# A hybrid decoder step: the first MLP product by seven block products in place of eight

## The chip, the core and the metric

The kernel runs on one core of one Trainium2 chip. TensorE (PE in the profile) multiplies, VectorE (DVE) and ScalarE (ACT) do the element-wise work, GpSimd (POOL) a little, and SyncE (SP) issues nearly all transfers. The metric is the time of one execution on the device in microseconds (us), the median of several runs.

## The reference

One layer of a decoder for 512 prompt tokens and 8 sample tokens that share the weights. What matters here, with all in fp32:

```python
u = rmsnorm(x, norm1_g) * (1 + sc1) + sh1
proj = u @ w_in                       # 1024 x 10272, split into nine sections
...
dt = softplus(dt_raw + dt_bias)       # dt_raw: 32 columns of proj
...
x = x + g1 * (merged @ w_o)
u2 = rmsnorm(x, norm2_g) * (1 + sc2) + sh2
hmid = square(relu(u2 @ w_mlp1))      # 1024 x 4096
x = x + g2 * (hmid @ w_mlp2)          # 4096 x 1024
y = rmsnorm(x, norm_f_g)
```

## The kernel before

**Layout.** Activations lie transposed: 128 features on the partitions, T = 520 tokens (512 prompt, 8 sample) along the row, so that a 1024-wide activation is eight tiles. A product goes by *windows*: one window computes one block of 128 output features for all 520 tokens, over eight blocks of 128 input features.

**Precision.** Each fp32 operand is split into a high part (fp32r, written by an ACT copy) and a low part (what is left, by a DVE subtraction): `wh`, `wl` for weights, `hi`, `lo` for activations. A product of two blocks is three matmuls: high by high, high by low, low by high. As 520 tokens are two halves of 260 columns (two PSUM banks), a window has 8 x 3 x 2 = 48 matmuls.

**Order.** Every engine works through its instructions in the order in which the program writes them; there is no scheduler. The main loop takes window `n` in four quarters `q` of 12 matmuls each. Around them it places the evacuation of window `n - 1` out of PSUM, the weight split of window `n + 2` (ACT copy, then DVE subtraction), and *hooks*: functions that `at(q, w, fn)` has put at a quarter of a window, and that `run` calls, sorted within one quarter by `PLAN["order"]`. Two two-bank accumulators (`mmtile`) are in rotation and four single banks (`aux`). Weights arrive in tiles of 1 MB for two windows (`load_w`, three buffers), issued on SP six windows ahead. Split weights have three buffers.

**The start.** Windows 0 to 3 compute sections B and C of the scan branch. An evacuation (`xbc_evac`) reads the accumulator twice on ACT (`raw`, `cv`) and runs a short convolution on DVE; a `finish` some windows later adds the sample columns (DVE) and applies SiLU (ACT). The softplus of `dt` is a chain of some fourteen small DVE instructions, `dt_b2`, hooked at the last quarter of window 3; `dt_b` comes before it, and `dt_c` (PE, ACT, DVE) in window 5 needs its result. `dt_b2` and the finish of window 2 stand in the same quarter, `dt_b2` first.

**The MLP** is in two halves of 2048 hidden features: sixteen windows `m1` (first product, then relu, square and split of the hidden tile), then sixteen windows `m2` (second product, two windows for each of eight output blocks, one accumulator; then `m2_evac` adds to the residual). The first nine `m1` windows use an input that isn't normalized yet, with nine more columns (270 in the second half of a row) that carry the shift; the others use `u3`, the normalized input that hooks prepare meanwhile (`make_u2`, `make_u2_lo`).

**The end.** The last output block is computed in two parts of the tokens, so that its residual, transposes (`finish_tile`), row sums (`last_rstd`) and stores overlap.

Of the kernel before, what the change touches and what calls it, by code (L numbers as in the profile page):

```python
# [8 lines left out]
F32 = mybir.dt.float32  # L9
# [8 lines left out]
P = 128  # L18
# [40 lines left out]
 'rstd': 11,  # L59
 'rstd_s': 17,  # L60
 'dt': [1, 3, 10],
 'u3': 9,
 'make_u2': 6,
 'lo_u2': 4,
 'hm': [1, 3],
 'last': [0, 2]}

# [5 lines left out]
def tile_hybrid_step(  # L73
# [32 lines left out]
    def act(name, dtype=F32):  # L106
        return ap.tile([P, SLOT], dtype, name=nm(name), tag="act", bufs=NSLOT)
# [4 lines left out]
    def small(shape, name):  # L112
        return sp.tile(shape, F32, name=nm(name), tag="small", bufs=4)
# [7 lines left out]
    def halves(ap_):  # L121
        return ap_.rearrange("p (h c) -> p h c", h=2)
# [16 lines left out]
    def a_copy(out, in_, func=AF.Copy, **kw):  # L139
        S.activation(out=out, in_=in_, func=func, **kw)  # L140

    def mm(out, lhsT, rhs, start=True, stop=True):
        PE.matmul(out, lhsT=lhsT, rhs=rhs, start=start, stop=stop)  # L143


    xa = {}
# [105 lines left out]
    def win(mat, r0, c0, i, xs, evac=None, first=True, last=True, n1=TH):  # L252
        wins.append(((mat, r0, c0), i, xs, evac, first, last, n1))
# [24 lines left out]
    def split_w(n):  # L278
# [8 lines left out]
            tt(lo, src, hi.bitcast(F32), ALU.subtract)  # L287
        rests.append(rest)

    def half(ps, h):  # L290
        return ps[h] if isinstance(ps, list) else ps[:, h, :]

    def product_part(ps, n, ks, h):
        hi, lo = splits[n]
        xs, first, last = wins[n][2](), *wins[n][4:6]
        c0, c1 = PART[h]
        for k in ks:
            xh, xl = xs[k]
            for i, (w_, x_) in enumerate(((hi, xh), (hi, xl), (lo, xh))):
                mm(ps[:, 0, 0:c1 - c0], w_[:, k, :], x_[:, c0:c1], first and k == 0 and i == 0,  # L300
                   last and k == KT - 1 and i == 2)

    def product(ps, n, ks):
# [17 lines left out]
    def at(q, w, fn, *args):  # L321
        hooks.setdefault(4 * w + q, []).append((fn, args))
# [242 lines left out]
    def rstd_small(v, n, r, rows=P):  # L565
        q = small([P, n], "q")[0:rows]
        a_copy(r, v, AF.Sqrt)
        V.reciprocal(out=r, in_=r)
        stt(q, r, -0.5, r, ALU.mult, ALU.mult)
        tt(q, q, v, ALU.mult)  # L570
        stt(r, q, 1.5, r, ALU.add, ALU.mult)
# [95 lines left out]
        mg.append(split(s))  # L667


    x2, u2, u3 = [], [], []  # L670
    sq2 = {}

    def residual(x_, xo, ps, prm, o):
# [33 lines left out]
        spread(rx, 1, 0, sq2[1])  # L707


    hm = []  # L710

    def make_u2(k):
        us, v, hi = small([P, NS], "us"), act("v2"), act("hi", F32R)
# [6 lines left out]
        a_copy(hi[:, 0:NP], v[:, 0:NP], AF.Identity, bias=mp(3, k))  # L720
        a_copy(hi[:, NP:T], v[:, NP:T])
        u3.append((v, hi))

    def make_u2_lo(k):
        v, hi = u3[k]
        lo = act("lo", F32R)
        stt(lo[:, 0:NP], v[:, 0:NP], mp(3, k), hi.bitcast(F32)[:, 0:NP], ALU.add, ALU.subtract)
        G.tensor_tensor(out=lo[:, NP:T], in0=v[:, NP:T], in1=hi.bitcast(F32)[:, NP:T], op=ALU.subtract)
        u3[k] = hi, lo

    def m1_evac(ps, w):
        if w >= W_U3:
            r = act("relu")
            a_copy(halves(r[:, 0:T]), ps[:, :, 0:TH], AF.Relu)
            at(PLAN["hm"][0], cur[0], m1_square, r)
            return
# [27 lines left out]
    def m2_evac(ps, w, o, half):  # L764
        residual(x2[o], x2[o], ps, 5, o)
        if half:
            if o == 0:
                sqf.insert(0, act("sqf"))
            add_square(sqf[0], x2[o], o == 0)
            if o == KT - 2:  # L770
                V.memset(vf, 1.0)
                at(end, w + 1, row_means, sqf, 1.0 / D, vf)
            at(mid, w + 1, finish_tile, o)

    sqf = []
    vf = const([P, 5], "vf")
    rf = const([P, 5], "rf")


    def last_evac(ps, h):  # L780
        o, (c0, c1) = KT - 1, PART[h]
        x_ = x2[o]
        stt(x_[:, c0:min(c1, NP)], ps[:, 0, 0:min(c1, NP) - c0], mp(5, o), x_[:, c0:min(c1, NP)])
        if not h:
            t = small([P, NS], "rs")
            tt(t, ps[:, 0, NP - c0:T - c0], msm(5, o), ALU.mult)
            tt(x_[:, NP:T], t, x_[:, NP:T], ALU.add)
            sqf.insert(0, act("sqf"))
        a_copy(sqf[0][:, c0:c1], x_[:, c0:c1], AF.Square)

    def last_rstd(h):
        cs = PART_C[h]
        row_means(sqf[0:1], 1.0 / D, vf, vf, cs)
        a, b = cs[0], cs[-1] + 1
        rstd_small(vf[:, a:b], b - a, rf[:, a:b])

    def last_out(h):
# [70 lines left out]
    W_U3 = W_M + PLAN["u3"]  # L868
# [75 lines left out]
    at(2, W_M, norm2_r)  # L944
    at(0, W_M + 1, norm2_b)
    for k in range(KT):
        at(PLAN["make_u2"] + 4 * k, W_M, make_u2, k)
        at(PLAN["make_u2"] + 4 * k + PLAN["lo_u2"], W_M, make_u2_lo, k)
    at(end, W_M + 4, load_g)

    cur = [0]
# [2 lines left out]
        firsts.setdefault(wn[0], n)  # L954
    load_order = sorted(firsts, key=lambda k: firsts[k])
    state = {"load": 2, "split": 3}

    def loads_to(n):
        while state["load"] < len(load_order) and firsts[load_order[state["load"]]] <= n:
# [1 line left out]
            state["load"] += 1  # L961

    def splits_to(n, whole=True):
        while state["split"] < NW and state["split"] <= n:
            split_w(state["split"])
            state["split"] += 1
        while whole and rests:
            rests.pop(0)()
# [270 lines left out]
        wins[n][3](ps_of.pop(n), n)  # L1239
        splits_to(3 + n)  # L1240
    dt_a()
    for n in range(3, NW - 2):
        cur[0] = n
        loads_to(n + 6)
        early = n < 40
        for q in range(4):
            if q == (1 if n == W_M + 1 else PLAN["evac" if early else "evac2"]) and wins[n - 1][3]:
                wins[n - 1][3](ps_of.pop(n - 1), n - 1)
            if q in PLAN["split" if early else "split2"]:
                splits_to(n + 2, q == PLAN["split" if early else "split2"][1])  # L1250
            if q == 0:
                ps_of[n] = mmtile("ps") if wins[n][4] else ps_of.pop(n - 1)
            product(ps_of[n], n, (2 * q, 2 * q + 1))
            for w in ([2, 3] if n == 3 and q == mid else [1, 2, 3] if n == 3 and q == end else [n]):
                run(w, q)


    cur[0] = NW - 2
    splits_to(NW - 1)
    wins[NW - 3][3](ps_of.pop(NW - 3), NW - 3)  # L1260
    for h in range(2):
        ps = mmtile("ps")
        for q in range(4):
            n = NW - 2 + q // 2
            product_part(ps, n, range(4 * (q % 2), 4 * (q % 2) + 4), h)
            run(NW - 2 + h, q)
            if h and q == PLAN["last"][0]:
                finish_tile(KT - 1, PART_C[0])
                last_rstd(0)
            if h and q == PLAN["last"][1]:  # L1270
                last_out(0)
        last_evac(ps, h)
    finish_tile(KT - 1, PART_C[1])
    last_rstd(1)
    last_out(1)

# [30 lines left out]
```

## Time and profile before

| | |
|---|---|
| three runs | 1166.93, 1167.24 (median), 1168.3 us |
| the profiled execution | 1167.75 us, of which 1165.9 us lie between the first and the last instruction (the span) |
| PE busy | 98% of the span, 9688 matmuls |
| DVE busy | 724.2 us, 62% |
| ACT busy | 448.2 us, 38% |
| DMA | 164.95 MB, mean 141 GB/s |
| granted clock of PE | 0.996 in the mean |

All rows come from that one execution. A row of the timeline gives the start, the time from the first start to the last end of so many like instructions, and in brackets how long the engine had been idle and what ended it. Like instructions overlap, so that the time of two is less than twice the time of one.

### The profile page before, as it was taken

Reading aid. Unit: us, or ns where it says so; the run is one execution under the profiler, and the core shown is the slowest. Engines: PE = TensorE matmul, PEld = TensorE weight load, DVE = VectorE, ACT = ScalarE, POOL = GpSimd, SP = SyncE. Lnnn points to the kernel's source line nnn. Section 1 sums busy time; section 2 is a strip of 40 time slices with the busy share of each in tenths; the row PEclk is TensorE's granted clock in tenths of the full one; section 3 lists DMA queues with packets and bytes.
Section 4 is the critical chain, followed back from the end, with each engine's and each line's share of the span. In section 5 each row is a group of like instructions: output and inputs, shape, how many; then the busy total and the mean of one; then the engine's idle time right before and its main releaser. Section 6 shows DMA issues by size and latency. Waiting matters only on the chain.

```text
span 1165.9 us, 22851 instructions
## 1 busy us (share of the span) xinstructions
PE 1142.0 (98%) x9688; PEld 1111.9 (95%) x9688; DVE 724.2 (62%) x1340; ACT 448.2 (38%) x666; POOL 42.4 (4%) x93
## 2 busy tenths in 40 slices
PE   7989999999999999999999999999999999999997
PEld 5789999999999888999999999999999999999997
DVE  5767888778888587888566333677743233444443
ACT  4446555455552222234443222345532113333222
POOL 3001111011110000000000000001000000000000
PEclk9989999999999999999999999999999999999999
DMA  9924333333348996566563243333322323232211
GB/s 284 321 73 132 114 114 96 93 112 114 114 141 283 333 324 201 181 187 198 183 229 100 97 163 122 115 123 101 100 73 90 117 85 108 74 109 73 73 37 74
DMA packets 137745, 164.95 MB, mean 141 GB/s; under 512 B 7144, under 2 KB 107961, under 8 KB 137636
## 3 DMA queue, kind: packets, MB, share of 16 engines
q1 hardware_dynamic: 137116, 162.85, 43.1%
q8 instruction: 76, 1.25, 0.4%
q0 software_dynamic: 528, 0.66, 0.2%
q14 instruction: 25, 0.20, 0.0%
HBM read 145.26 MB, written 18.45 MB: 140 GB/s over the span
## 4 chain that ended last, share of the span: by engine, by line
PE 94%; DMA 3%; DVE 1%; SPq 1%; ACT 1%; issue 0%; ACTq 0%; DVEq 0%
PE ps L143 86%; DMA wa<-in_w_ada_dram 2%; PE pada L143 1%; PE pyd L143 1%; PE pst L143 1%; PE pyo L143 1%; PE ptx L411 1%; SPq L215 0%; DMA xa<-in_x_prompt_dram 0%; PE pcb L143 0%; DMA wt<-in_w_in_dram 0%; PE pdt L143 0%; PE pt L817 0%; ACT cv L140 0%; PE pq L143 0%
## 5 line engine op out<-in xcount | busy, mean ns | idle before, releaser
L143 PE MATMUL ps<-hi,wh 128*128 128x260 f32 (+2 forms) x2816 | 579.2, 286 | 5.6 <-ACT cv L140 5.0
L143 PE MATMUL ps<-lo,wh 128*128 128x260 f32 (+2 forms) x2816 | 570.9, 283 | 1.7 <-DVE lo L128 1.4
L143 PE MATMUL ps<-hi,wl 128*128 128x260 f32 (+2 forms) x2816 | 568.9, 282 | 0.0
L143 PEld LDWEIGHTS ps<-hi,wh 128*128 128x128 f32 x2816 | 435.4, 189 | 20.1 <-issue 13.2
L143 PEld LDWEIGHTS ps<-lo,wh 128*128 128x128 f32 x2816 | 436.6, 189 | 3.3 <-DVE lo L128 3.3
L143 PEld LDWEIGHTS ps<-hi,wl 128*128 128x128 f32 x2816 | 435.5, 188 | 0.0
L140 ACT ACTIVATE wh<-wt 128x1024 fp32r<-128x1024 f32 (+1 forms) x179 | 186.5, 1043 | 412.0 <-PE ps L143 400.4
L128 DVE TENSOR_TENSOR wl<-wt,wh 128x1024 fp32r<-128x1024 f32 (+1 forms) x179 | 215.5, 1205 | 170.2 <-ACT wh L140 170.0
L131 DVE SCALAR_TENSOR_TENSOR cv<-raw,par,cv 128x511 f32<-128x511 f32 (+2 forms) x72 | 54.0, 751 | 11.9 <-ACT cv L140 9.9
L128 DVE TENSOR_TENSOR rs<-ps,mod 128x8 f32<-128x8 f32 x24 | 4.0, 166 | 62.5 <-PE ps L143 62.5
L140 ACT ACTIVATE hi<-relu 128x520 fp32r<-128x520 f32 x32 | 20.5, 640 | 42.7 <-DVE relu L128 42.7
L397 POOL TENSOR_SCALAR_AFFINE_SELECT seg<-seg 128x512 f32<-128x512 f32 x32 | 24.8, 796 | 302.8 <-DVE seg L128 250.4
L140 ACT ACT_TABLE_LOAD x27 | 34.6, 1283 | 2.9 <-DVE cv L131 1.7
L128 DVE TENSOR_TENSOR lo<-relu,hi 128x520 fp32r<-128x520 f32 x32 | 22.4, 700 | 16.4 <-ACT hi L140 16.4
L140 ACT ACTIVATE cv<-cv 128x520 f32<-128x520 f32 x24 | 15.3, 638 | 44.2 <-DVE cv L131 44.2
L143 PE MATMUL pada<-wa,cT 128*32 128x128 f32 (+1 forms) x384 | 26.7, 386 | 1.2 <-DMA wa<-in_w_ada_dram 1.0
L128 DVE TENSOR_TENSOR seg<-seg,cbm 128x512 f32<-128x512 f32 x32 | 20.7, 689 | 10.0 <-ACT seg L140 10.0
L140 ACT ACTIVATE seg<-seg 128x512 f32<-128x512 f32 x32 | 19.5, 632 | 17.6 <-POOL seg L397 17.6
L140 ACT ACTIVATE hf<-pyo 128x128 f32<-128x128 f32 x16 | 4.4, 277 | 54.1 <-DVE e L128 54.1
L131 DVE SCALAR_TENSOR_TENSOR hn<-hn,sdec,t 128x512 f32<-128x512 f32 x32 | 24.1, 752 | 1.1
L128 DVE TENSOR_TENSOR s<-ps,sgr 128x520 f32<-128x520 f32 x8 | 5.6, 700 | 29.0 <-PE ps L143 29.0
L128 DVE TENSOR_TENSOR t<-hn,swk 128x512 f32<-128x512 f32 x32 | 22.1, 692 | 1.1
(278 smaller groups left out, 825.3 us busy)
## 6 DMA issues: line engine op xcount, KB each, us to landing
wt<-in_w_in_dram SPq DMA_DIRECT2D x38, 1024.0 KB
wt<-in_w_mlp_dram SPq DMA_DIRECT2D x32, 1024.0 KB
wa<-in_w_ada_dram SPq DMA_DIRECT2D x96, 256.0 KB
acb<-ascr SPq DMA_DIRECT2D x32, 256.0 KB
hn<-in_state_ssm_dram SPq DMA_DIRECT2D x32, 256.0 KB
out_dram<-hn SPq DMA_DIRECT2D x32, 256.0 KB
wt<-in_w_b_out_dram SPq DMA_DIRECT2D x8, 1024.0 KB
gscr<-sg SPq DMA_DIRECT2D x16, 260.0 KB
```

The lines of the kernel that those rows point to most:

```text
L128: V.tensor_tensor(out=out, in0=in0, in1=in1, op=op)
L131: V.scalar_tensor_tensor(out=out, in0=in0, scalar=scalar, in1=in1, op0=op0, op1=op1)
L140: S.activation(out=out, in_=in_, func=func, **kw)
L143: PE.matmul(out, lhsT=lhsT, rhs=rhs, start=start, stop=stop)
L397: G.affine_select(out=sv, in_=sv, pattern=[[0, NC], [1, P]], compare_op=ALU.is_ge, fill=-1e30, base=0, channel_multiplier=-1)
L411: PE.transpose(ptx[:, c * P:(c + 1) * P], xT_[:, c * P:(c + 1) * P], ident)
```

## The change

Three things are changed.

**The MLP goes in quarters** of 1024 hidden features: eight windows `m1`, eight windows `m2`, each `m2` window one whole output block (so 32 evacuations into the residual in place of 16). The first quarter's `m1` uses the input that isn't normalized, in eight windows. The first two windows of each `m2` are interleaved (`two`).

**In the other three quarters, two `m1` windows at a time are one 2x2 block product by seven products** (`seven`, Strassen's scheme in Winograd's form). The two rows of blocks are the two output blocks; the inner dimension is cut in two halves of four input blocks; the columns are the two halves of the tokens. DVE forms four sums of weight blocks (`split_s`, in four units for each pair) and, once, four sums of the activations (`make_terms`, hooked into the first quarter's windows, with their splits in `split_terms`). A product is 4 x 3 = 12 matmuls of 260 columns. The seven use three banks; four of them add onto a bank that still holds an earlier product, which ACT or DVE has read in the meantime. The rest of the sums is done as the banks are read.

**`dt_b2` is sorted behind the other hooks of its quarter.** At the end of the kernel, the last two windows are now two output blocks, each in two parts of the tokens.

```diff
- 'order': {'scan3': 2, 'scan2': 5, 'scan1': 5, 'scan_w': -2, 'scan_m': 5},
+ 'order': {'dt_b2': 9, 'scan3': 2, 'scan2': 5, 'scan1': 5, 'scan_w': -2, 'scan_m': 5},
...
+    def split_s(n, t):
+        w = tiles[wins[n][0]]
+        (a11, a21), (a12, a22) = ([w[:, 4 * r:4 * r + 4, i * P:(i + 1) * P] for i in range(2)] for r in range(2))
...
+        if t == 0:
+            total(1, a21, a22, ALU.add)
+            total(2, sums[1], a11, ALU.subtract)
+        elif t == 2:
+            total(3, a11, a21, ALU.subtract)
+            total(4, a12, sums[2], ALU.subtract)
+        src = ((a11, sums.get(2)), (sums.get(1), a12), (sums.get(3), sums.get(4)), (a22,))[t]
...
+        for i, x in enumerate(src):
+            a_copy(hi[:, 4 * i:4 * i + 4], x)
+
+        def rest():
+            for i, x in enumerate(src):
+                tt(lo[:, 4 * i:4 * i + 4], x, hi.bitcast(F32)[:, 4 * i:4 * i + 4], ALU.subtract)
+        rests.append(rest)
...
+    def make_terms(j):
...
+        tt(c[:, TH:T], b[:, TH:T], a[:, TH:T], ALU.subtract)
+        tt(a[:, TH:T], a[:, TH:T], a[:, 0:TH], ALU.subtract)
+        tt(c[:, 0:TH], b[:, TH:T], a[:, TH:T], ALU.subtract)
+        tt(d, b[:, 0:TH], c[:, 0:TH], ALU.subtract)
...
-    for hf_ in range(2):
-        for q in range(16):
-            late = len(wins) >= W_U3
-            win("m1", 0, 2048 * hf_ + 256 * (q // 2), q % 2, lambda v=u3 if late else u2: v, m1_evac,
-                n1=TH if late else SLOT - TH)
+    for f in range(4):
+        for q in range(8):
+            if f and q % 2 == 0:
+                pairs.add(len(wins))
+            win("m1", 0, 1024 * f + 256 * (q // 2), q % 2, lambda: u2, None if f else m1_evac, n1=SLOT - TH)
+        twos.add(len(wins))
         for k in range(KT):
-            for a in range(2):
-                win("m2", 2048 * hf_ + D * a, 256 * (k // 2), k % 2, lambda a=a, h=hf_: hm[16 * h + 8 * a:16 * h + 8 * a + 8],
-                    (lambda ps, w, k=k, h=hf_: m2_evac(ps, w, k, h)) if a else None, a == 0, a == 1)
+            win("m2", D * f, 256 * (k // 2), k % 2, lambda f=f: hm[8 * f:8 * f + 8],
+                lambda ps, w, k=k, f=f: m2_evac(ps, w, k, f == 3))
...
+    def seven(n):
+        yx, wb = mmtile("yx"), aux("wb")
+        y, x, w = yx[:, 0, 0:TH], yx[:, 1, 0:TH], wb[:, 0:TH]
+        banks = (y, x, w, y, x, w, x)
...
+        def squares(r, hi, c0):
+            a_copy(r[:, c0:T], r[:, c0:T], AF.Relu)
+            a_copy(r[:, 0:T], r[:, 0:T], AF.Square)
+            a_copy(hi[:, 0:T], r[:, 0:T])
+
+        def after(p):
+            if p == 0:
+                a_copy(s1, y)
+                while later:
+                    later.pop(0)()
+                evac(n - 1)
+            elif p == 1:
+                tt(u2_, x, s1, ALU.add)
+            elif p == 2:
+                tt(s15[:, 0:TH], w, s1, ALU.add)
+            elif p == 3:
+                a_copy(r0[:, 0:TH], y, AF.Relu)
+            elif p == 4:
+                tt(r1[:, TH:T], x, s15[:, 0:TH], ALU.add)
+            elif p == 5:
+                tt(r0[:, TH:T], w, u2_, ALU.add)
+                squares(r0, hl[0][0], TH)
+            else:
+                tt(r1[:, 0:TH], x, s1, ALU.add)
+                m1_lo(r0, *hl[0])
+                squares(r1, hl[1][0], 0)
+                later.append(lambda: m1_lo(r1, *hl[1]))
+
+        for p in range(7):
+            splits_to(unit_of[n] + p // 2 + 2, p % 2 == 1)
+            (hi, lo), c = splits[n, p // 2], 4 * (p % 2)
+            for k in range(4):
+                xh, xl = terms[p][k]
+                for i, (w_, x_) in enumerate(((hi, xh), (hi, xl), (lo, xh))):
+                    mm(banks[p], w_[:, c + k, :], x_, p < 3 and k == 0 and i == 0, k == 3 and i == 2,
+                       skip_group_check=True)
+            after(p)
+            run(n + p // 4, p % 4)
+        splits_to(unit_of[n] + 5)
+        run(n + 1, 3)
...
     def last_rstd(h):
-        cs = PART_C[h]
-        row_means(sqf[0:1], 1.0 / D, vf, vf, cs)
+        cs, pq = PART_C[h], aux("pq")
         a, b = cs[0], cs[-1] + 1
+        for c in cs:
+            m = P if c < NC else NS
+            for i in range(2):
+                mm(pq[0:m, c:c + 1], sql[i][:, c * P:c * P + m], ones[:, 0:1], i == 0, i == 1)
```

## Rows read from the trace of the kernel before

**Rows 1.** The page's first part: busy time of each engine.

```profile
PE 1142.0 (98%) x9688; PEld 1111.9 (95%) x9688; DVE 724.2 (62%) x1340; ACT 448.2 (38%) x666; POOL 42.4 (4%) x93
```

**Rows 2.** The chain of waits from 843 us: start, duration, what.

```profile
842.96 230.48 PE ps L143 x1926
```

**Rows 3.** Busy time by stretch: PE, PEld, DVE, ACT, POOL, clock, DMA share, GB/s.

```profile
876.00:969.00 93.00, 93.00 (x779) 93.00 (x778) 30.79 (x51) 18.21 (x19) 0.00 (x0) 1.00 0.32 103
969.00:1063.00 94.00, 94.00 (x788) 94.00 (x788) 41.18 (x49) 35.06 (x48) 0.00 (x0) 1.00 0.26 81
```

**Rows 4.** Timeline of PE, two places between 74 and 122 us.

```profile
77.78 0.80 PE L143 MATMUL ps<-hi,wh 128*128 128x260 f32 x2 [5.01 <-ACT cv L140]
...
102.64 1.05 PE L143 MATMUL pst<-xdec,btok 128*128 128x128 f32 x8
```

**Rows 5.** Busy time by stretch around two idle times of PE; columns as above.

```profile
5.20:7.15 1.95, 0.01 (x2) 0.01 (x1) 0.00 (x0) 1.93 (x4) 1.88 (x6) 1.00 0.95 290
...
72.80:77.80 5.00, 0.02 (x1) 0.02 (x1) 3.04 (x12) 1.88 (x4) 0.00 (x0) 0.92 0.01 1
77.80:84.00 6.20, 6.20 (x29) 6.20 (x30) 4.38 (x8) 3.35 (x6) 0.00 (x0) 0.51 0.57 171
```

**Rows 6.** Groups by shape: count, busy us, mean ns, idle before and releaser.

```profile
L140 ACT ACTIVATE wh<-wt 128x512 fp32r<-128x512 f32 x6 | 3.5, 618 | 0.0
L140 ACT ACTIVATE sqf<-x 128x264 f32<-128x264 f32 x1 | 0.4, 424 | 6.2 <-DVE x L128 6.2
L128 DVE TENSOR_TENSOR wl<-wt,wh 128x512 fp32r<-128x512 f32 x6 | 3.9, 686 | 0.0
L128 DVE TENSOR_TENSOR e<-pyo,e 128x384 f32<-128x384 f32 x16 | 8.9, 557 | 1.7 <-PE pyo L442 1.5
```

**Rows 7.** Timeline of ACT and of DVE between 21 and 62 us.

```profile
34.23 1.13 ACT L140 ACTIVATE wh<-wt 128x512 fp32r<-128x512 f32 x2
61.06 0.38 ACT L140 ACTIVATE raw<-ps 128x260 f32<-128x260 f32 x1
21.03 1.29 DVE L128 TENSOR_TENSOR wl<-wt,wh 128x512 fp32r<-128x512 f32 x2
```

**Rows 8.** Groups by shape in the MLP, 779 to 1166 us.

```profile
L143 PE MATMUL ps<-hi,wh 128*128 128x260 f32 x96 | 19.3, 282 | 0.0
L140 ACT ACTIVATE hi<-relu 128x520 fp32r<-128x520 f32 x32 | 20.5, 640 | 42.7 <-DVE relu L128 42.7
L128 DVE TENSOR_TENSOR lo<-relu,hi 128x520 fp32r<-128x520 f32 x32 | 22.4, 700 | 16.4 <-ACT hi L140 16.4
L131 DVE SCALAR_TENSOR_TENSOR x<-ps,mod,x 128x520 f32<-128x520 f32 x15 | 11.4, 759 | 0.5
```

**Rows 9.** Timeline of DVE, 55 to 122 us.

```profile
71.20 0.68 DVE L128 TENSOR_TENSOR sm<-sm 128x160 f32<-128x160 f32 x2
...
75.67 0.22 DVE L131 SCALAR_TENSOR_TENSOR cv<-raw,par,pb 128x8 f32<-128x8 f32 x1
...
77.76 2.32 DVE L131 SCALAR_TENSOR_TENSOR cv<-raw,par,cv 128x511 f32<-128x511 f32 x3 [0.99 <-ACT cv L140]
...
100.58 0.69 DVE L128 TENSOR_TENSOR xdec<-ptx,dd 128x512 f32<-128x512 f32 x1
```

**Rows 10.** Timeline of ACT, 55 to 95 us.

```profile
75.92 0.64 ACT L140 ACTIVATE cv<-cv 128x520 f32<-128x520 f32 x1 [4.84 <-DVE cv L131]
...
76.95 0.78 ACT L140 ACTIVATE cv<-ps,par,par 128x520 f32<-128x520 f32 x1
...
87.95 0.59 ACT L140 ACTIVATE at<-pat 32x512 f32<-32x512 f32 x1 [1.32 <-PE pat L143]
...
90.38 1.05 ACT L140 ACTIVATE wh<-wt 128x1024 fp32r<-128x1024 f32 x1
```

**Rows 11.** Timeline of PE at the end: the row sums of the last block.

```profile
1152.07 0.63 PE L143 MATMUL pq<-ones,sqf 128*128 128x1 f32 x6
...
1158.18 0.61 PE L143 MATMUL pq<-ones,sqf 128*128 128x1 f32 x4
```

More of the change, by code (lines that the diff above doesn't have):

```diff
@@ L61 @@
  'dt': [1, 3, 10],
- 'u3': 9,
+ 'terms': 12,
+ 'terms_split': [34, 6],
  'make_u2': 6,
- 'lo_u2': 4,
  'hm': [1, 3],
@@ L140, in a_copy, with mm @@
         S.activation(out=out, in_=in_, func=func, **kw)
-    def mm(out, lhsT, rhs, start=True, stop=True):
-        PE.matmul(out, lhsT=lhsT, rhs=rhs, start=start, stop=stop)
+    def mm(out, lhsT, rhs, start=True, stop=True, **kw):
+        PE.matmul(out, lhsT=lhsT, rhs=rhs, start=start, stop=stop, **kw)
     xa = {}
@@ L707, in norm2_b @@
         spread(rx, 1, 0, sq2[1])
-    hm = []
+    hm, td = [], []
+    terms = [[None] * 4 for _ in range(7)]
     def make_u2(k):
-        us, v, hi = small([P, NS], "us"), act("v2"), act("hi", F32R)
+        us, v = small([P, NS], "us"), act("v2")
         rb, x_ = sq2[1], x2[k]
@@ L719, in make_u2, with split_terms @@
         stt(v[:, 0:NP], x_[:, 0:NP], mp(4, k), rb[:, 0:NP], ALU.mult, ALU.mult)
[L720 to L729, printed above, removed]
-    def m1_evac(ps, w):
[L732 to L736, printed above, removed]
+        a_copy(v[:, 0:NP], v[:, 0:NP], AF.Identity, bias=mp(3, k))
+        u3[k] = v
+    def make_terms(j):
+        a, b, c = u3[j], u3[j + 4], act("tc")
+        if j % 2 == 0:
+            td.append(act("td"))
+        d = td[-1][:, TH * (j % 2):TH * (j % 2) + TH]
+        tt(c[:, TH:T], b[:, TH:T], a[:, TH:T], ALU.subtract)
+        tt(a[:, TH:T], a[:, TH:T], a[:, 0:TH], ALU.subtract)
+        tt(c[:, 0:TH], b[:, TH:T], a[:, TH:T], ALU.subtract)
+        tt(d, b[:, 0:TH], c[:, 0:TH], ALU.subtract)
+        u3[j + 8] = c
+    def split_terms(j):
+        parts = [(u3.pop(j), (0, j), (2, j)), (u3.pop(j + 4), (3, j), (5, j)), (u3.pop(j + 8), (1, j), (4, j))]
+        if j % 2:
+            parts.append((td[j // 2], (6, j - 1), (6, j)))
+        for v, *where in parts:
+            hi, lo = split(v)
+            for h, (i, k) in enumerate(where):
+                terms[i][k] = hi[:, h * TH:(h + 1) * TH], lo[:, h * TH:(h + 1) * TH]
+    def m1_evac(ps, w):
         sh, r = small([P, 9], "sh"), act("relu")
@@ L946, in tile_hybrid_step @@
     for k in range(KT):
-        at(PLAN["make_u2"] + 4 * k, W_M, make_u2, k)
-        at(PLAN["make_u2"] + 4 * k + PLAN["lo_u2"], W_M, make_u2_lo, k)
+        at(PLAN["make_u2"] + 4 * k, W_M, make_u2, k // 2 + 4 * (k % 2))
+    for j in range(4):
+        at(PLAN["terms"] + 8 * j, W_M, make_terms, j)
+        at(PLAN["terms_split"][0] + PLAN["terms_split"][1] * j, W_M, split_terms, j)
     at(end, W_M + 4, load_g)
@@ L956, in tile_hybrid_step @@
     state = {"load": 2, "split": 3}
+    units, unit_of = [], {}
+    for n in range(NW):
+        if n not in pairs and n - 1 not in pairs:
+            unit_of[n] = len(units)
+            units.append((n,))
+        elif n in pairs:
+            unit_of[n] = len(units)
+            units += [(n, t) for t in range(4)]
     def loads_to(n):
@@ L963, in splits_to @@
     def splits_to(n, whole=True):
-        while state["split"] < NW and state["split"] <= n:
-            split_w(state["split"])
+        while state["split"] < len(units) and state["split"] <= n:
+            u_ = units[state["split"]]
+            split_w(*u_) if len(u_) == 1 else split_s(*u_)
             state["split"] += 1
@@ L1241, in tile_hybrid_step, with evac, one @@
     dt_a()
-    for n in range(3, NW - 2):
-        cur[0] = n
-        loads_to(n + 6)
+    later = []
+    def evac(n):
+        if wins[n][3]:
+            wins[n][3](ps_of.pop(n), n)
+    def one(n):
         early = n < 40
         for q in range(4):
-            if q == (1 if n == W_M + 1 else PLAN["evac" if early else "evac2"]) and wins[n - 1][3]:
-                wins[n - 1][3](ps_of.pop(n - 1), n - 1)
+            if q == (1 if n == W_M + 1 else PLAN["evac" if early else "evac2"]):
+                evac(n - 1)
             if q in PLAN["split" if early else "split2"]:
-                splits_to(n + 2, q == PLAN["split" if early else "split2"][1])
+                splits_to(unit_of[n] + 2, q == PLAN["split" if early else "split2"][1])
             if q == 0:
@@ L1255, in tile_hybrid_step, with two @@
                 run(w, q)
+    def two(n):
+        for i in range(8):
+            w, q = (n + i // 3, i % 3) if i < 6 else (n + i - 6, 3)
+            if i in (0, 1, 7):
+                splits_to(unit_of[n] + (3 if i == 7 else 2), i > 0)
+            if q == 0:
+                ps_of[w] = mmtile("ps")
+            product(ps_of[w], w, (2 * q, 2 * q + 1))
+            if i == 0:
+                while later:
+                    later.pop(0)()
+                evac(n - 1)
+            if i == 6:
+                evac(n)
+            run(n + i // 4, i % 4)
@@ new lines, in seven @@
+    def seven(n):
+        yx, wb = mmtile("yx"), aux("wb")
+        y, x, w = yx[:, 0, 0:TH], yx[:, 1, 0:TH], wb[:, 0:TH]
+        banks = (y, x, w, y, x, w, x)
+        su, s15, r0, r1 = act("su"), act("s15"), act("relu"), act("relu")
+        s1, u2_ = su[:, 0:TH], su[:, TH:T]
+        hl = [(act("hi", F32R), act("lo", F32R)) for _ in range(2)]
+        def squares(r, hi, c0):
[5 more added lines that the diff above has]
+                a_copy(s1, y)
+                while later:
+                    later.pop(0)()
+                evac(n - 1)
+            elif p == 1:
[26 more added lines that the diff above has]
+        run(n + 1, 3)
@@ L1258, in tile_hybrid_step @@
+    n = 3
+    while n < NW - 2:
+        cur[0] = n
+        loads_to(n + 6)
+        (seven if n in pairs else two if n in twos else one)(n)
+        n += 2 if n in pairs or n in twos else 1
     cur[0] = NW - 2
-    splits_to(NW - 1)
-    wins[NW - 3][3](ps_of.pop(NW - 3), NW - 3)
+    splits_to(len(units) - 1)
+    evac(NW - 3)
     for h in range(2):
```

48 lines of the change are left out of this document (31 added, 17 removed).

## The prediction

> **What bounds the kernel now.** I read the share of each engine first: PE is busy for 98% of the span [rows 1]. The reader is to see that only work taken off PE, or a wait taken out of it, can shorten this kernel. The chain of waits says the same of the MLP: from 843 us on, one unbroken piece of 230.48 us is 1926 matmuls of PE, with no other engine in it [rows 2]. That is 0.1197 us for each matmul of 260 columns, 1.436 us for twelve, 5.75 us for a window of 48. The table by stretch shows what covers it: in the second half's first product (969 to 1063 us) DVE is busy for 41.18 us of 94 and ACT for 35.06, in the second product before it (876 to 969) for 30.79 and 18.21 of 93 [rows 3]. So there is room on both, but the change spends it. Last I looked for holes in PE, and there is one large one, at 72.8 to 77.8 us: the timeline of PE shows 5.01 us of waiting for an ACT result named cv [rows 4], and the table by stretch shows the granted clock at 0.51 (the lower of the two levels, 1.2 GHz) for the 6.2 us behind it [rows 5].
>
> **Part one: seven products for eight.** Twelve pairs of windows lose 96 - 84 = 12 matmuls each: 144 x 0.1197 = 17.2 us less on PE [rows 2]. Each matmul has its own weight load before and after, so I keep the spacing. The Trainium skill ("TensorE: Matmul & The Clock Gate", Back-to-back issue gap) gives columns / 2.4 plus 2.5 ns, which would be 110.8 ns and 16.0 us in place of 17.2; the row shows 119.7 ns, and the row decides.
>
> What the pair adds to the other two engines, by rows of the same shapes. A half-window weight block (128x512) costs ACT 0.62 us and DVE 0.69 [rows 6]; back to back they start 0.51 and 0.60 apart (1.13 and 1.29 for two) [rows 7]. A sum of 260 columns on DVE isn't in the trace; 512 take 0.686 and 384 take 0.557, so by that slope 260 take 0.43 [rows 6], 0.35 back to back. A 520-column pass takes 0.64 on ACT and 0.70 on DVE [rows 8], 0.54 and 0.61 back to back. DVE per pair: four weight sums and seven low parts (11 x 0.60), five sums out of PSUM (5 x 0.35), two low parts of the hidden tiles (2 x 0.61) = 9.6 us, where seven products last 10.05. ACT: seven copies, one copy and one relu out of PSUM, one relu of half a tile, five passes of 520 columns = 7.2 us. Both fit as totals; the order in their queues is what I cost.
>
> Count from the start of the fourth product (p3), which adds onto the bank of the first and so must wait until ACT has copied that (s1). ACT issues in program order: relu, square and copy of r0 (after the sixth product, p5); two weight copies; relu, square and copy of r1; two weight copies of the next pair's third unit; only then s1. After p5, at 3 x 1.436 = 4.31, the last matmul is readable 0.16 later (0.282 long against a spacing of 0.12 [rows 8]), and a reader starts 0.03 after that (DVE's cv ends at 75.89, ACT's starts at 75.92 [rows 9, 10]): 4.50. DVE comes late to the sum that starts r0: behind s1 it still has one low part of weights until 0.52, then sums and low parts of 0.35 + 0.35 + 0.60 + 1.32 (the second weight sum needs the first) + 0.35 + 1.20, so it starts at 4.69 and ends at 5.12. Then ACT: 0.45 (half-tile relu; 264 columns take 0.424 [rows 6]) + 0.67 + 0.54 + 1.02 + 0.67 + 0.67 + 0.54 + 1.02 + 0.38 (260 columns out of PSUM [rows 7]) = 5.96. s1 ends at 5.15 + 5.96 = 11.11, p3 can start at 11.16, and seven products take 10.05: **PE waits 1.1 us in each pair**. The first pair of a quarter finds ACT idle and waits for nothing, the second about 1.0: 3.2 us in each quarter, 9.6 in three. Bounds: 0.6 a pair if dependent ACT passes overlap as independent ones do (four overlaps and their gaps, some 0.5), 1.5 if each of the dozen hand-overs costs 0.03 more. I take 1.1, from the rows' own spacing. Behind the late product nothing else is late: the weights of the next products have been ready for a product or more by then.
>
> **Smaller parts of the MLP.** One window at 270 columns becomes one at 260: -0.2. The second product is evacuated sixteen times more, 0.76 us of DVE each and three small ones [rows 8]; in that stage DVE has 62 us of 93 idle [rows 3], and the accumulator is free again before PE needs it two windows later, so I cost it at nothing (12 us and more if DVE were full). The terms (sixteen sums of 0.43, fourteen splits of 0.64 on ACT and 0.70 on DVE, less eight low parts) have the thirteen windows, 75 us, before their first use: nothing either; uncovered they would be 20. Weight loads stay at one MB for two windows; the tile is released at the pair's fourth product instead of a window ahead, with two further tiles in flight. The tail gains a row sum for one more tile: six and four single-column matmuls become twelve and eight, which take 0.63 and 0.61 us now, some 0.16 of each the last one's own length beyond its slot [rows 11]: 0.47 + 0.45, +0.9, half of it at the very end.
>
> **Part two: the softplus series.** Before, DVE runs the series from 71.20 and only at 75.67 the conv finish behind it [rows 9]; ACT stands idle 4.84 us for that, and the evacuation that PE waits for sits behind it in ACT's queue [rows 10]. After, the finish goes at 71.20, its activation at 71.45, the evacuation ends at 73.3 instead of 77.7. PE's wait shrinks by 4.5 us, and if the clock stays up the 6.2 us at 0.51 give 3.0 back [rows 5]: 7.4 at most. But DVE has the same work; its next convolution starts at 76.7 in place of 77.76 [rows 9], 1.1 earlier. ACT then loses the 1.32 us in which it waited for PE at 87.95, so its weight copy of 90.38 comes 2.6 earlier [rows 10], and so does xdec, which ends at 101.27 and is needed by PE at 102.64 [rows 4, 9]. There PE can be only 2.6 + 1.4 = 4.0 early; what it won beyond that it waits off again. I take 3.8 (2.6 if that slack is used up further on, 7.4 if DVE catches up). On SP's queue the series' four small transfers and the weight load behind them come 1 us later; that load feeds a window over 20 us away.
>
> **Sum.** -17.2 + 9.6 - 0.2 + 0.9 - 3.8 = -10.7 against the profiled execution's own 1167.75 us: 1157.0. The runs' median is 0.5 under it, which I neglect. A difference under 0.2% (2.3 us) can't be told from none.
>
> **Rivals.** *The cover holds* (0.24): ACT's passes are shorter, or s1 isn't last, and PE never waits in a pair. For it: both totals fit in 10.05 us. Against: a strict chain of eleven ACT instructions stands between p5 and s1, and [rows 10] show ACT holding a ready evacuation behind one late activation. -17.2 - 0.2 + 0.9 - 3.8: 1147. *Seven are no faster than eight* (0.15): DVE at 9.6 of 10.05 and ACT's chain lock into a period of 11.5 us, a wait of 1.44 in all twelve pairs; for it the thin margin, against it the idle first pair. Only -3.1 is left: 1164. *The clock falls* (0.09, slower): each of nine waits of 1.1 us is followed by a stretch at 1.2 GHz like that of 77.8 to 84.0, at 3.0 us each [rows 5]: +27, 1184; from four such pairs on, the gain of 10.7 is gone. Against it: PE sat idle 1.94 us at 5.2 to 7.15 and the granted clock stayed at 1.00 there; it fell after 5.0 us. The Trainium skill ("TensorE: Matmul & The Clock Gate", Why this matters for your kernels) warns of idle gaps between bursts in the middle of a kernel for just this reason; by that rule waits that recur in every pair are the risk, and the trace shows it for one gap and not for the shorter one.
>
> **How the numbers follow.** Forecast 0.52, rivals 0.24, 0.15 and 0.09. The forecast's own range is 1151 to 1161 (waits of 0.6 to 1.5 in nine pairs, 2.6 to 7.4 for the series). To hold the time 8 times in 10 the range takes in most of the first two rivals: 1146 to 1164. Faster 0.89 (the forecast, the first rival and most of the second), same 0.03, slower 0.08.
>
> **What would show it.** In the changed profile: 144 fewer MLP matmuls at 0.12; in pairs two to four of each quarter PE idle about 1.1 us before the fourth product, released by ACT's su, with ACT nearly dense from r0's relu on, and none in the first pair; granted clock 1.00 there; at 72.8 us a hole of half a microsecond instead of 5.0, but new waits of 1 to 3 us in PE before 100 us; the first pst about 4 us earlier. I am wrong if waits sit elsewhere (low parts from DVE, a PSUM bank held by a late sum), if the pairs run without any, or if PE keeps the full 7 us of the hole.

## The result, and the profile after

The changed kernel takes 1220.88 us (median of four runs, 1220.51 to 1221.89) against 1167.51 for the kernel before: a ratio of 1.046, 95% interval 1.0447 to 1.0473. It is 53.4 us slower. The forecast was 1157.0 us, a gain of 10.7; even the slow rival (1184) fell 37 us short.

PE has its 134 matmuls fewer, and yet it is no longer always busy:

```profile
PE 1153.8 (95%) x9554; PEld 1116.1 (91%) x9554; DVE 812.0 (67%) x1566; ACT 498.3 (41%) x780; POOL 46.0 (4%) x85
```

Against [rows 1] the span has grown by 54 us and PE's share has gone from 98% to 95%. The waits of PE by what ended them (total us, times, longest):

```profile
PE yx L143 <- ACT su L140: 35.9, 12, 3.8
...
PE yx L143 <- ACT relu L140: 5.7, 12, 0.5
```

That is 41.6 us in twelve pairs, and the place is the surprise. The timeline of PE in the first quarter with pairs shows each wait:

```profile
876.51 0.39 PE L143 MATMUL yx<-hi,wh 128*128 128x260 f32 x1 [0.48 <-ACT su L140]
881.58 0.39 PE L143 MATMUL yx<-hi,wh 128*128 128x260 f32 x1 [0.48 <-ACT relu L140]
891.42 0.39 PE L143 MATMUL yx<-hi,wh 128*128 128x260 f32 x1 [3.83 <-ACT su L140]
898.01 0.39 PE L143 MATMUL yx<-hi,wh 128*128 128x260 f32 x1 [0.48 <-ACT relu L140]
907.87 0.59 PE L143 MATMUL yx<-hi,wh 128*128 128x260 f32 x1 [3.83 <-ACT su L140]
```

The wait for `su` (the copy s1) stands one product after the start of the pair, not three: before p1, which writes the bank `x`. Before p3, which adds onto the copied bank `y`, there is none any more. And p4, which adds onto `x`, waits 0.48 us for the relu that reads `y`. Both products wait for ACT to finish with a bank that they don't touch. `y` and `x` are the two halves of one tile, `yx`, and the program orders accesses by tile.

ACT's queue is as the prediction had it, from the relu of r0 to s1 as its last (the timeline of ACT; six instructions between are left out):

```profile
918.97 1.09 ACT L140 ACTIVATE relu<-relu 128x260 f32<-128x260 f32 x2 [2.69 <-DVE relu L128]
...
923.54 1.13 ACT L140 ACTIVATE wh<-ss 128x512 fp32r<-128x512 f32 x2
924.58 0.36 ACT L140 ACTIVATE su<-yx 128x260 f32<-128x260 f32 x1
```

From the start of the half-tile relu to the end of s1 are 5.97 us; the prediction's chain of eleven instructions came to 5.96. The length was right, the instruction that waits for it was not: p1 stands two products (2.87 us) ahead of p3, so a wait of 1.1 becomes one of about 4.

A second loss lies on top. Busy time by stretch (PE, PEld, DVE, ACT, POOL, granted clock, DMA share, GB/s) over a pair, a stretch of a second product, and the start of one pair:

```profile
907.00:925.00 18.00, 12.83 (x84) 12.42 (x84) 10.93 (x20) 8.83 (x18) 0.00 (x0) 0.78 0.19 59
960.00:980.00 20.00, 20.00 (x169) 20.00 (x168) 11.21 (x25) 4.19 (x6) 0.00 (x0) 1.00 0.24 80
1108.90:1111.50 2.60, 2.52 (x11) 2.53 (x12) 0.76 (x2) 0.02 (x1) 0.00 (x0) 0.50 0.00 0
```

After the long wait PE runs at 0.50, the level of 1.2 GHz: p1 takes 2.97 us in place of 1.44, as the chain of waits shows:

```profile
907.87 2.97 PE yx L143 x12
```

A pair takes 17.13 us (907.87 to 925.00), where two windows took 11.5. In the stretch of a second product PE is busy throughout and the clock is 1.00, as in [rows 3].

The series part did what its step said, and less than its size: PE's wait of 5.01 us for the evacuation [rows 4] has shrunk to 0.56, and xdec is waited for instead.

```profile
74.90 0.51 PE L143 MATMUL ps<-hi,wh 128*128 128x260 f32 x2 [0.56 <-ACT cv L140]
...
100.39 2.04 PE L143 MATMUL pst<-xdec,btok 128*128 128x128 f32 x8 [2.22 <-DVE xdec L128]
```

### The profile page after: what moved, and what is told of

Read it like the earlier page. It is cut to its first block, busy times and chain, and to the rows that moved or that the text cites. A ratio compares the mean times of both kernels' runs of the same rounds, so it can differ in the third digit from the quotient of the medians.

```text
span 1220.1 us, 22943 instructions
## 1 busy us (share of the span) xinstructions
PE 1153.8 (95%) x9554; PEld 1116.1 (91%) x9554; DVE 812.0 (67%) x1566; ACT 498.3 (41%) x780; POOL 46.0 (4%) x85
## 4 chain that ended last, share of the span: by engine, by line
PE 85%; ACT 6%; DVE 4%; DMA 3%; issue 1%; SPq 1%; ACTq 0%; DVEq 0%
PE ps L143 69%; PE yx L143 6%; PE wb L143 2%; DMA wa<-in_w_ada_dram 2%; ACT relu L140 2%; ACT wh L140 2%; PE pada L143 1%; PE pyd L143 1%; PE pst L143 1%; DVE wl L128 1%; PE pyo L143 1%; ACT hi L140 1%; DVE cv L131 1%; DVE relu L128 1%; PE ptx L439 1%
## 5 line engine op out<-in xcount | busy, mean ns | idle before, releaser
L143 PE MATMUL ps<-hi,wh 128*128 128x260 f32 (+2 forms) x2432 | 502.0, 287 | 2.4 <-ACT cv L140 1.1
L143 PE MATMUL ps<-lo,wh 128*128 128x260 f32 (+2 forms) x2432 | 493.5, 283 | 1.7 <-DVE lo L128 1.4
L143 PE MATMUL ps<-hi,wl 128*128 128x260 f32 (+2 forms) x2432 | 490.9, 282 | 0.0
L143 PEld LDWEIGHTS ps<-hi,wh 128*128 128x128 f32 x2432 | 375.4, 188 | 18.1 <-issue 13.6
L143 PEld LDWEIGHTS ps<-lo,wh 128*128 128x128 f32 x2432 | 376.7, 188 | 3.3 <-DVE lo L128 3.3
L143 PEld LDWEIGHTS ps<-hi,wl 128*128 128x128 f32 x2432 | 376.1, 188 | 0.0
L143 PE MATMUL yx<-hi,wh 128*128 128x260 f32 x240 | 75.5, 315 | 41.6 <-ACT su L140 35.9
L143 PE MATMUL yx<-lo,wh 128*128 128x260 f32 x240 | 72.5, 302 | 0.0
L143 PE MATMUL yx<-hi,wl 128*128 128x260 f32 x240 | 72.5, 302 | 0.0
L143 PEld LDWEIGHTS yx<-hi,wl 128*128 128x128 f32 x240 | 50.2, 209 | 0.0
```

The source lines that it names most:

```text
L143: PE.matmul(out, lhsT=lhsT, rhs=rhs, start=start, stop=stop, **kw)
```

## The experiments

Times are medians; ratios are against the kernel before, run on the same chip.

**1. y in a tile of its own.** Nothing else differs from the changed kernel.

```diff
-        yx, wb = mmtile("yx"), aux("wb")
-        y, x, w = yx[:, 0, 0:TH], yx[:, 1, 0:TH], wb[:, 0:TH]
+        yb, xb, wb = aux("yb"), mmtile("xb"), aux("wb")
+        y, x, w = yb[:, 0:TH], xb[:, 0, 0:TH], wb[:, 0:TH]
```

> The first and second bank of a pair lie in two tiles instead of two halves of one. Theory A (the second product waits for ACT's copy of the first only because accesses to a two-bank tile are ordered as if it were one): no wait before the second and the fifth product, a wait of about 1.0 us before the fourth in pairs two to four of each quarter, granted clock 1.00 in the pairs; a quarter's four pairs take 43.4 us in place of 62.8, so 1163 us. Rival B (the copy is late for whoever needs it, and the tile has nothing to do with it): the waits of 3.8 us stay, 1215 to 1221 us. Rival C (as A, but waits of 1 us lower the clock too): 3 us more in each of nine pairs, 1190 us.

Measured: 1163.11 us, ratio 0.9963 (0.9948 to 0.9977): 57.8 us less than the change, from this edit alone. The shared tile was the cause. What is left is the wait that the prediction described, before p3 and in pairs two to four alone:

```profile
PE yb L143 <- ACT su L140: 8.1, 9, 0.9
```

**2. The series alone**, in the kernel before.

```diff
- 'order': {'scan3': 2, 'scan2': 5, 'scan1': 5, 'scan_w': -2, 'scan_m': 5},
+ 'order': {'dt_b2': 9, 'scan3': 2, 'scan2': 5, 'scan1': 5, 'scan_w': -2, 'scan_m': 5},
```

> The kernel before with the softplus series behind the other hooks and nothing else. Theory A (DVE and ACT have the same work, so PE wins only what their queues win): 2.5 to 3.8 us less than before, 1164 us. Rival (PE keeps the hole and the slow clock that it saves): 7.4 less, 1160. Rival (the series only moves the wait): 1167.5, no difference.

Measured: 1165.23 us, ratio 0.9977 (0.9967 to 0.9986), some 2.4 us less than before and just short of theory A's 2.5 to 3.8. The same 2.22 us of waiting for xdec end at 98.25 us, and in the six us behind them the granted clock is 0.72 (columns as above):

```profile
98.00:104.00 6.00, 5.75 (x35) 5.76 (x36) 4.57 (x8) 3.83 (x7) 2.23 (x4) 0.72 0.19 39
```

The product behind xdec (`pst`) starts 4.4 us earlier than before (98.25 against 102.64 [rows 4]), near the 4.0 that the prediction allowed. The lower clock behind it takes back some 1.7 us (six us at 0.72).

**3. s1 ahead of the third unit's weight copies**, with the shared tile: the call that splits this unit moves from before p0 to behind its `after(0)`.

```diff
         for p in range(7):
-            splits_to(unit_of[n] + p // 2 + 2, p % 2 == 1)
+            if p:
+                splits_to(unit_of[n] + p // 2 + 2, p % 2 == 1)
...
             after(p)
+            if not p:
+                splits_to(unit_of[n] + 2, False)
```

> The changed kernel, with ACT's copy of the first product issued ahead of the two weight copies of the third unit, the banks still in one tile. Theory A (the wait before the second product is the length of ACT's queue ahead of that copy): the wait of 3.83 us shrinks by the two copies, to 2.9, and moves nowhere; nine times 0.9 less, 1212 us if 2.9 us still lower the clock, 1190 us if they don't. Rival (the weight copies become the late ones): 1221 us, with a wait before the fifth product.

Measured: 1203.84 us, ratio 1.0311 (1.0292 to 1.033). The wait before p1 falls from 3.83 to 2.79 us, 9.4 us in nine pairs; the other 7.6 are the clock's, by this subtraction. The chain of waits has p1 and p2 of three pairs, each behind a wait of 2.79 us:

```profile
889.38 2.97 PE yx L143 x12
892.35 2.60 PE wb L143 x12
...
905.94 2.97 PE yx L143 x12
908.90 1.56 PE wb L143 x12
...
921.19 1.76 PE yx L143 x12
922.96 2.60 PE wb L143 x12
```

At full clock each would take 1.44 us, or some 1.7 right behind a wait. The clock is down for p1 and p2, for p1 alone, and for p2 alone: it still falls, but less is lost than after 3.83 us, where p1 and p2 were both slow. After one of the nine waits it didn't fall at all (1.00 from 1009.9 to 1013.0 us). So the time lies between the two numbers expected.

**4. Work in the gap**: in the changed kernel, twelve products with the identity (24 matmuls, 2.9 us, results unused) between p0 and p1 of pairs two to four.

```diff
+            if p == 0 and n - 2 in pairs:
+                pw = aux("pw")
+                for _ in range(12):
+                    mm(pw[:, 0:P], ident, ident)
             after(p)
```

> The changed kernel with twelve unused products of the identity by itself (24 matmuls, 2.9 us) on PE between the first and the second product of pairs two to four of each quarter, where PE waits anyway. Theory A (the wait costs twice: itself, and about 2.4 us behind it in which PE runs at 1.2 GHz): the clock stays at 1.00 and nine times 2.4 us go, 1199 us. Rival (the slow clock hides under the waits of the other engines): 1221 us.

Measured: 1199.49 us, ratio 1.0275 (1.026 to 1.0291), mean granted clock 0.998 against 0.973 in the changed kernel. The same s1 is waited for, 2.9 us of the wait are now filled with useless work, and the kernel is 21.4 us faster: that is the price of the clock, 2.4 us for each of the nine long waits. p1, behind the 1.15 us of waiting that are left, is back to 1.70 us:

```profile
902.80 1.70 PE yx L143 x12
904.50 1.44 PE wb L143 x12
```

**5. y in its own tile, and s1 first**, with the edit of experiment 3. The tile of its own had left a question: its chain of waits runs through pairs two to four without coming to PE. One pair of it, from one square of r0 to the next (the pieces between left out):

```profile
893.66 0.65 ACT relu L140
...
897.79 1.14 ACT wh L140 x2
898.92 0.28 ACT su L140
...
899.24 0.69 DVE wl L128
...
902.86 1.20 DVE wl L128 x2
904.06 0.35 DVE relu L128
...
904.89 0.65 ACT relu L140
```

ACT works for 5.5 us, then DVE for 5.2, then ACT again: 11.23 us a pair, where PE needs 10.08.

> As the kernel with y in a tile of its own (1163.1 us), and the copy s1 also put ahead of the third unit's two weight copies on ScalarE. Theory wait: in that kernel nine pairs lost 0.90 us of waiting before the fourth product plus 0.27 us of slower restart each, because s1 stood behind those two copies (1.14 us); with s1 first the loss goes, nine times 1.17 = 10.5 us, and the time is about 1152.6 us. Theory loop: in pairs 2 to 4 the chain of waits runs for 30 us through ScalarE and VectorE alone and never through TensorE (a stretch of 5.5 us of VectorE, then 5.8 us of ScalarE, each beginning where the other ends), so 11.23 us a pair is the period of this loop; then s1 first moves the wait to another place (the products that wait for weights or for the bank x) and the time stays at 1162 to 1164 us.

Measured: 1179.69 us, ratio 1.0109 (1.0093 to 1.0125): outside both. The wait before p3 is down to 0.7 us in all, and 16.0 us of waiting have come before p4, for DVE's `su` (the sum u2). Moving the split call had also moved the two weight sums that it issues on DVE: they now stand behind the low part of r1, which waits for ACT, and ACT's weight copies wait for them. The clock fell as well, after five of the nine waits: the timeline has one such p4, and the table by stretch what came behind it.

```profile
901.24 0.36 PE L143 MATMUL xb<-hi,wh 128*128 128x260 f32 x1 [1.79 <-DVE su L128]
```
```profile
901.20:906.00 4.80, 4.76 (x27) 4.79 (x28) 3.80 (x8) 0.77 (x2) 0.00 (x0) 0.64 0.56 192
```

The run speaks against the theory of a mere wait, but it moved two things; experiment 10 moves only one.

**6. The quarters and the end alone**: all windows `m1` by eight products, no `seven` and no terms. The hooks that prepare the normalized input and the terms go too (these lines are left out below).

```diff
-            if f and q % 2 == 0:
-                pairs.add(len(wins))
-            win("m1", 0, 1024 * f + 256 * (q // 2), q % 2, lambda: u2, None if f else m1_evac, n1=SLOT - TH)
+            win("m1", 0, 1024 * f + 256 * (q // 2), q % 2, lambda: u2, m1_evac, n1=SLOT - TH)
...
```

> The MLP in quarters, with the end and the series as in the changed kernel, but every window of the first product by eight products and none by seven; the sums of inputs for the seven are left out, nothing of the reference is. It prices the quarters and the end alone. The series alone gave 1165.2 us; 23 more windows with 270 columns in place of 260 add 0.16 us each, 3.7 us. Theory nothing else: 1168.9 us. Theory end: the own-tile kernel gained 2.1 us over the series alone where 17.2 less 10.5 would be 6.7, so quarters and end cost 4.6 us more: 1173.5 us, with the waits of the last quarter's transposes for VectorE and the longer tail visible here too.

Measured: 1173.03 us, ratio 1.005 (1.0035 to 1.0066), as theory "end" had it. Its chain of waits shows what the end has gained: four steps in which PE stands still for DVE in the last output blocks, where the series alone has one (at 1154.69 us, 0.49).

```profile
1147.04 0.48 DVE x L131
...
1153.68 0.50 DVE yo L128 x2
...
1157.18 0.50 DVE x L131
...
1160.87 0.50 DVE x L131
```

**7. Two weight sums on GpSimd**, the third and fourth of each pair, on top of experiment 5.

```diff
-            tt(sums[i], x, y, op)
+            if i > 2:
+                G.tensor_tensor(out=sums[i], in0=x, in1=y, op=op)
+            else:
+                tt(sums[i], x, y, op)
```

> As e6, and two of the four weight sums of each pair (the third and fourth) on GpSimd in place of VectorE, which takes 1.26 to 1.30 us out of VectorE's stretch of each pair. Theory wait: nothing more to gain over e6, both 1152 to 1153 us. Theory loop: e6 stays near 1163 us, and here the loop shortens from 11.23 to about 10 us a pair, below TensorE's 10.08: 1153 to 1155 us. If GpSimd's sums are slow (its 128x512 operation took 0.80 us elsewhere in this trace) or hold up VectorE, the weight copy that needs them comes late and the time is above e6's.

Measured: 1177.28 us, ratio 1.0086 (1.0068 to 1.0104). Neither theory's number. The timelines of POOL and of DVE over the same 3 us:

```profile
894.36 1.29 POOL L299 TENSOR_TENSOR ss<-wt,ss 128x512 f32<-128x512 f32 x1 [10.45 <-DVE ss L128]
895.61 1.75 POOL L299 TENSOR_TENSOR ss<-wt 128x512 f32<-128x512 f32 x1
```
```profile
894.47 1.73 DVE L128 TENSOR_TENSOR wl<-wt,wh 128x512 fp32r<-128x512 f32 x1
896.12 1.78 DVE L128 TENSOR_TENSOR wl<-ss,wh 128x512 fp32r<-128x512 f32 x1
```

While GpSimd sums, a DVE subtraction that takes 0.69 us otherwise [rows 6] takes 1.73 to 1.78: it ends 0.5 to 0.6 us after GpSimd's instruction does. The Trainium skill ("SBUF — State Buffer", SBUF: two separate sides) says that GpSimd and a VectorE operation with two inputs in SBUF take a shared pair of ports in turns, whoever starts first for its whole instruction. By that rule DVE's subtractions stand still while GpSimd sums, and the trace agrees: 1.26 us of sums left DVE in a pair, and in this one 2.1 us of blocking came. Over all twelve pairs the 84 subtractions of this size took 70.7 us, against 56.6 in experiment 5: 1.2 us more a pair, so that DVE gained nothing. That the time is still 2.4 us under experiment 5 goes with the granted clock (0.997 in the mean against 0.991); no run took the two apart.

**8. The second unit's copies early** (on top of experiment 1): the next pair's second unit is split ahead of the squares of r0, and its low parts are taken ahead of r0's.

```diff
             tt(r0[:, TH:T], w, u2_, ALU.add)
+            splits_to(unit_of[n] + 5, False)
             squares(r0, hl[0][0], TH)
         else:
+            splits_to(unit_of[n] + 5)
             tt(r1[:, 0:TH], x, s1, ALU.add)
```

> As the kernel with y in a tile of its own (1163.1 us), with one step moved: the weight copies and rests of the next pair's second unit, which stood behind ScalarE's work on both squares, now stand ahead of the squares of r0, and their two rests on VectorE ahead of the low part of r0. Theory loop: in pairs 2 to 4 VectorE works without a break for 9.4 us, from the low part of one r0 to the sum for the next r0, and then waits 1.8 us while ScalarE does relu, square and copy of that r0: 11.23 us a pair. With 1.2 us of the 9.4 moved into that gap the loop takes 10.1 to 10.4 us, TensorE's own 10.08 or a little over, and nine pairs give 7.5 to 10 us: 1153 to 1156 us; the wait before the fourth product is gone or a few tenths. Theory ScalarE's order: the wait before the fourth product is the place of s1 in ScalarE's queue and nothing else; here the squares of r0 start 1.0 us later and s1 comes no earlier, so 1163 us or more.

Measured: 1157.65 us, ratio 0.9911 (0.9895 to 0.9928). The gap in which DVE waits for ACT's copy of r0 is filled with the two low parts of weights:

```profile
892.91 0.69 DVE L128 TENSOR_TENSOR wl<-ss,wh 128x512 fp32r<-128x512 f32 x1
893.52 0.68 DVE L128 TENSOR_TENSOR wl<-wt,wh 128x512 fp32r<-128x512 f32 x1
894.12 0.42 DVE L128 TENSOR_TENSOR relu<-xb,su 128x260 f32<-128x260 f32 x1
895.09 0.70 DVE L128 TENSOR_TENSOR lo<-relu,hi 128x520 fp32r<-128x520 f32 x1 [0.54 <-ACT hi L140]
```

A pair takes 10.60 us (887.69 to 898.29, the starts of two p3) and the wait before p3 is 0.26. The loop theory holds, though the gain was 5.5 us and not 7.5 to 10. ACT copies weights at the end of p5 already, where it waited 1.25 us for DVE's sum before, so from the end of p5 to the end of s1 are 6.0 us in place of 6.6. The chain of waits now runs through ACT and PE, and no longer through DVE.

**9. The end too**: in the last quarter the transposes of the second output tile also go to the end of their window.

```diff
-            at(mid if o else end, w + 1, finish_tile, o)
+            at(mid if o > 1 else end, w + 1, finish_tile, o)
```

> As e9, and in the last quarter the transposes of the second output tile also go to the end of their window in place of its middle, so that they are not asked for while VectorE still works on the first. If the 1.5 us of waiting before them (seen in the own-tile kernel and in the quarters alone) is a loss of the path, it goes and the time is 1.2 to 1.7 us below e9's; if it only moves to the next window's transposes or the tail, the same as e9.

Measured: 1155.88 us, ratio 0.9898 (0.9884 to 0.9913), against 0.9911 in the same batch. The 1.5 us before the transposes are gone from PE's waits. The difference of 1.8 has the size expected, but the two intervals overlap.

**10. Experiment 5 with DVE's order kept**: s1, then the split call, then the low part of r1. ACT gets s1 first; DVE's queue is as in experiment 1.

```diff
             if p == 0:
                 a_copy(s1, y)
+                splits_to(unit_of[n] + 2, False)
                 while later:
                     later.pop(0)()
...
         for p in range(7):
-            splits_to(unit_of[n] + p // 2 + 2, p % 2 == 1)
+            if p:
+                splits_to(unit_of[n] + p // 2 + 2, p % 2 == 1)
```

> As the kernel with y in a tile of its own (1163.1 us), with only s1 ahead of the third unit's copies on ScalarE and VectorE's order left as it is: the earlier run of s1 first (1179.7 us) with its one slip mended, the two sums of VectorE that had come behind the low part of r1. Theory loop: 11.23 us a pair is VectorE's loop through ScalarE, and s1 in front of the third unit's copies lengthens ScalarE's way to VectorE's rests by 0.27 us: the time stays at 1162 to 1166 us, the wait before the fourth product gone and another of the same size in its place. Theory wait: 1152.6 us. In both the 16.6 us that the earlier run lost go, if the place of the two sums was their cause.

Measured: 1163.05 us, ratio 0.996 (0.9945 to 0.9975): no gain over experiment 1. PE's waits have only moved, most of them to p4:

```profile
PE xb L143 <- ACT relu L140: 2.8, 5, 0.6
PE xb L143 <- DVE su L128: 2.3, 4, 0.6
...
PE yb L143 <- ACT su L140: 1.0, 6, 0.2
```

p4 needs DVE's u2, which reads the bank `x`; the relu to which five of its waits are put down ended within 0.01 us of u2 in the pairs at 891 and 903 us. The chain of waits still runs through ACT and DVE alone, with 11.32 us from one relu of r0 to the next:

```profile
895.65 0.43 ACT relu L140
...
906.97 0.43 ACT relu L140
```

So the wait before p3 was a symptom. The loop of ACT and DVE set the pace, and the 16.6 us of experiment 5 came from the place of the two sums.

**11. All of it**: experiment 9 with the order of experiment 10.

> As the kernel of the last run (1155.9 us: y in a tile of its own, second unit's copies early, transposes of the second output tile late), and the copy s1 ahead of the third unit's two weight copies on ScalarE, with VectorE's order left as it is (its two weight sums still ahead of the low part of r1, which the earlier run of s1 first had turned round). Before the fourth product that kernel still waits 0.26 us and restarts 0.27 us slower in nine pairs. Theory: VectorE's loop is now shorter than TensorE's 10.08 us, so the wait goes and nine times 0.53 = 4.8 us with it: 1151 us. Rival: VectorE (9.8 us busy a pair) is the next bound, the pair stays at 10.3 us or more, and the wait moves to the weights or the bank x: 1153.5 to 1156 us.

Measured: 1153.84 us, ratio 0.9883 (0.9866 to 0.9899). Now that DVE no longer sets the pace, s1 first removes the wait before p3. The chain of waits shows p1 and p4 of one pair and p1 of the next, 10.37 us later, and the table by stretch the engines over this time:

```profile
894.78 1.43 PE xb L143 x12
...
899.16 1.68 PE xb L143 x12
...
905.15 1.43 PE xb L143 x12
```
```profile
894.78:905.15 10.37, 10.30 (x87) 10.12 (x86) 9.86 (x19) 7.93 (x16) 0.00 (x0) 1.00 0.32 103
```

The chain of waits is PE's again, but for a short stop before p4 (1.68 us in place of 1.44). DVE is busy for 9.86 of the 10.37 us. This version beats both kernels: 1.2% under before, 5.5% under the change as it was made.

## Why the prediction was wrong

**The step that failed** is the one that places the wait: the fourth product "adds onto the bank of the first and so must wait until ACT has copied that (s1)". It took for granted that only products on the same bank wait. The products wait by tile, and `yx` is one tile with two banks, so p1 waits for s1, and p4 for the relu of y. The line that makes the tile stands in the diff; what was missing is the question what else lies in the tile that a reader holds. None of the rows read from the kernel before shows two users of one tile's halves at cross purposes, so the cost should have been bounded from both sides, as other unseen costs were, and should have stood among the rivals.

The Trainium skill ("PSUM — Partial Sum Buffer", PSUM bank collisions raise a hardware error) asks for guards by bank and quadrant, and not by address. By that rule PE may write one bank while ACT reads the other; experiment 1 agrees, where p1 waits no more. The wait was the program's choice, not the chip's.

**Point by point.**

| step | predicted | measured |
|---|---|---|
| 144 matmuls | -17.2 | -17.0: a pair without waits takes 10.08 us (experiment 1, 872.54 to 882.62) against 11.5, twelve times |
| wait before p3, nine pairs | +9.6 | +10.5 with y in its own tile: 0.90 us of waiting and 0.27 of slower restart each |
| one window narrower, tail | +0.7 | about 4: 1173.0 - 1165.2 in experiment 6 less some 4 for 23 wider windows; by subtraction in experiment 1, 4.6 |
| series | -3.8 | -2.4 (experiment 2) |
| the shared tile | none | +58, experiment 1 against the change |

The first four give 1163, and experiment 1 is there. The 58 are 33.5 us of waiting (41.6 less 8.1), 21.4 of clock (experiment 4), and some 3 left. I put these down to the restarts: the change has 24 waits in its pairs, experiment 1 has nine, and fifteen restarts of 0.26 us would be 3.9 (an argument, no run).

- **The chain on ACT** was right to 0.01 us, as the timeline after shows, and the first pair of a quarter does find ACT idle.
- **The rival "the clock falls"** came about, and gave the larger part of its price per wait (2.4 us, 3.0 forecast). It was held unlikely because a wait of 1.1 us lay below every gap after which the clock had fallen. With the right place of the wait the gap is 3.83, between the 1.94 after which the clock had stayed up and the 5.01 after which it had fallen [rows 5], and the rival would have weighed far more. The rule of the Trainium skill that stands beside it ("TensorE: Matmul & The Clock Gate", Why this matters for your kernels) warned of the risk that came about.
- **The rival "seven are no faster than eight"** had the right mechanism in a smaller size: DVE and ACT do lock into a period, of 11.23 us and not 11.5, in three pairs of four. What I called a wait for s1 was this loop (experiments 8 and 10): my chain had the half of it that lies on ACT, and DVE's late sum at its start, and its length came out right.
- **The tail** was under-counted: it had only the row sums. Two output blocks that end together also put three more hand-overs from DVE into PE's way, and the transposes wait behind the first evacuation.
- **The series**: the bound at xdec was seen, but not that the clock would fall behind the new wait there (0.72 in experiment 2).

## What to carry to other kernels

Before costing a wait, ask which object the program orders by: here two banks in one tile were one object, and the second product waited for the reader of the first. When a chain of waits runs through two engines without coming to the one that is busiest, the loop between them is the period, and taking away the wait that PE shows only renames it; first fill the gap in the loop. An edit that moves a call moves what it issues on every engine.

## What the runs showed of the hardware

- The length of a wait did not by itself decide whether PE's clock fell. It fell after all nine waits of 3.83 us in the changed kernel (0.50 in the stretch shown), after eight of nine waits of 2.79 (experiment 3), and after five of nine waits of 1.75 to 1.79 (experiment 5: 0.64 over the 4.8 us behind the one shown, 1.00 over the 4.8 us behind the 1.77 at 888.73). It stayed at 1.00 after the nine waits of 0.90 in experiment 1, and after the 1.94 us of [rows 5] (1.00 from 7.15 to 9.00 us). What decides between these was not tried.
- Filling a gap with useless matmuls gave back 21.4 us, though the result that PE waits for came no earlier: the granted clock stayed up.
- A restart costs something by itself: the twelve matmuls behind a wait of 0.26 (experiment 8) to 1.15 us (experiment 4) took 1.69 to 1.72 us in place of 1.44, at full clock.
- A GpSimd sum of 128x512 (1.29 to 1.75 us) stretched a DVE subtraction beside it from 0.69 to 1.73 us and more; GpSimd needs about twice DVE's time for the sum itself.
